# The lag between GpSimd's product and ScalarE's cast in the stick-breaking branch, from 1.5 to 3.0 units

## The chip, the cores and the metric

The kernel runs on one core of a Trainium2 chip. A core has five engines that work side by side, each through its own queue in order: TensorE (PE in the profile; its weight loads are listed as PEld), VectorE (DVE), ScalarE (ACT), GpSimd (POOL) and SyncE (SP), whose queue here issues nearly all DMAs. TensorE writes its results to PSUM, eight banks of 128 x 512 float32; the other data lie in SBUF. The metric is the time of one execution in device microseconds (us), as the median of several runs.

## The reference

One layer of a streaming encoder, for 2048 new frames of one stream (the prompt: 16 tiles of 128 rows) and 16 next frames of each of 8 running streams (the sample: one more tile of 128 rows, with 512 cached positions per stream). After an RMS norm with a conditioning vector, one wide matrix product makes queries, keys, values and gates for two attention branches. Branch A is a differential softmax attention with 4 heads; branch B is a stick-breaking attention with 8 heads of width 64. Both outputs are gated, projected and summed, and a last projection and norm follow. The lines that matter here are those of branch B:

```python
z = einsum('bqhd,bkhd->bhqk', q, k) * HEAD_DIM_B ** -0.5
mask = kpos[None, :] < qpos[:, None]
log_1m = where(mask, log_sigmoid(-z), 0.0)
log_a = log_sigmoid(z) + cumsum(log_1m, axis=3, reverse=True) - log_1m
a = where(mask, exp(log_a), 0.0)
o = einsum('bhqk,bkhd->bqhd', a, v)
```

So the weight of key k for query q is sigmoid(z) at k, times the product of sigmoid(-z) over all later keys that the query may see. The kernel computes it in that form: two sigmoids, a running product from the right, and one multiplication. Results are float32; matrix operands are split into two float16 halves, high and low, and multiplied in two or three passes.

## The kernel before

**Stages.** A first stage makes the modulated input (to about 80 us). Then come eight units: unit u has branch A for even u and branch B for odd u, and the pair u // 2 of heads (one wide head of A, two heads of B). A unit has 17 tiles: the sample's tile first (it is only projected here, and scored in the last stage), then the 16 prompt tiles in order. For each tile there is a projection (24 matmuls of 128 x 512 in 12 pieces, L467; in odd units another 24 for the gates, L543) and the scores against all keys up to the tile's own, in chunks of 512 keys (L708, L709, with the mask L712 on the last chunk). A last stage, from about 1770 us, gates, projects and stores, and scores the sample's tile beside that.

**One head of branch B in one tile.** `scores` (L694) goes through the chunks from the right. TensorE makes a chunk of z in one of three banks of PSUM that carry the tag s. ScalarE makes sigmoid(z) into the buffer sc_p and sigmoid(-z) in place in PSUM (`evacuate`, L606 and L607; by their helper, the profile has them at L134). VectorE scans sigmoid(-z) from the right into sc_n (`stick`, L682), which ends the chunk's use of the bank. A head's keys are cut into segments of up to 1024 (SEG blocks of 128): one segment in tiles 0 to 7, two in tiles 8 to 15. When the last chunk of a head has been scanned, `stick_weights` (L684) is called, first for the later segment if there are two, then for the other:

- GpSimd multiplies sc_p by the shifted sc_n into sc_p (L688, "GpSimd's product");
- `turn` (L609) follows, called some time later: ScalarE casts sc_p to float16 into sc_n's room (L616, "the cast"), VectorE subtracts that cast from sc_p to get the low half (L619, "the subtraction"), and SP issues a DMA that transposes both halves into a buffer wt (L626);
- `turn` also dates the products of these weights with the values on TensorE (`pv`, L779: L769 and L770 for branch B, L765 to L767 for branch A), 27 units (PV_LAG) after itself; the last of them for a tile ends with `natural` (L738; its last product on GpSimd is L752) and a store of the output.

There are six buffers sc_p and six sc_n (SC_BUFS), five wt (WT_BUFS), and 23 tiles of values (V_BUFS), shared by both branches. Branch A uses the same `turn` from `softmax_pair` (L632), with lags of its own (TURN_LAG, EXP_LAG, SUM_LAG).

**What sets the order.** The main loop (L1417) goes through (unit, tile) steps. For each it lists pieces of projections, about five tiles ahead (LEAD), the chunks of scores, and side work (loads and splits of the next unit's weights, sums over the caches), mixes the three lists by their costs, and hands them to `give` (L796). `give` calls one piece after another and adds its cost to a counter of the work that TensorE has been given: 0.44 (PIECE) for a projection piece of two matmuls, twice 0.22 (CHUNK) for a full chunk, 0.085 (PV_B) for a block of the weights' product in branch B. `later_on(lag, fn)` puts a function on a list that is sorted by counter + lag, and `give` calls it when the counter has got there:

```python
def later_on(lag, fn, cost=0.0):
    spent[1] += 1
    bisect.insort(due, (spent[0] + lag, spent[1], cost, fn))
...
    fn()
    spent[0] += weight * costs[i]
    while due and due[0][0] <= spent[0]:
        _, _, cost, product = due.pop(0)
        product()
        spent[0] += cost
```

So a lag counts work given to TensorE in program order, not time. The program is then handed to a scheduler that fixes each engine's queue when the program is built, by an estimate of the times; it may move an instruction ahead of others of its engine, except where the program asks for its order to be kept. The cast of the units before the last is kept in that way (L617, L618), and activations that go through the helper `act` keep their order among themselves. The subtraction and the DMA are not kept.

Unit 7 and the sample's tile call `turn` at once after the product, with no lag (L689).

Of the kernel before, what the change touches and what calls it, by code (L numbers as in the profile page):

```python
# [39 lines left out]
SEG = 8  # L40
PV_LAG = 27.0
TURN_LAG = 1.5
B_LAG = 1.5
EXP_LAG = 1.0
SUM_LAG = 2.0
PIECE, CHUNK, PV_A, PV_B = 0.44, 0.22, 0.17, 0.085
# [78 lines left out]
def layer_kernel(ctx: ExitStack, tc: tile.TileContext, a: dict):  # L125
# [483 lines left out]
    def turn(job, seg, scale=None):  # L609

        nb = seg["hi"] - seg["lo"]
        nk = nb * P
        w16 = seg["n"].bitcast(F16)
        hi, lo, src = w16[:, 0:nk], w16[:, nk : 2 * nk], seg["p"][:, 0:nk]
        if scale is None:
            x = S.copy(out=hi, in_=src)  # L616
            if job["t"] < NT and job["U"]["u"] < 7:  # L617
                kept(x)  # L618
            V.tensor_tensor(out=lo, in0=src, in1=hi, op=ALU.subtract)  # L619
        else:  # L620
            split(hi, lo, src, scale, S)
        if job["t"] == NT:
            seg["wt"] = job["pool"].tile([P, 10, P], F16, tag="dwt", name="dwt", bufs=2)
        else:
            seg["wt"] = wtp.tile([P, 2 * SEG, P], F16, tag="wt", name="wt", bufs=WT_BUFS)
        nc.sync.dma_start_transpose(out=seg["wt"][:, 0 : 2 * nb, :], in_=w16[:, 0 : 2 * nk])  # L626
        if job["t"] < NT:
            cost = (PV_A, PV_B)[job["U"]["kind"]]
            for fn in pv(job, seg):
                later_on(PV_LAG, fn, cost)  # L630
# [54 lines left out]
    def stick_weights(job, seg, later):  # L685
# [5 lines left out]
        else:  # L691
            later_on(B_LAG + m / 1024, lambda: turn(job, seg))

# [80 lines left out]
# [4 lines that stand above are left out]
# [858 lines left out]
```

## Time and profile before

| | |
|---|---|
| median of 3 runs | 2220.72 us (2216.34 to 2229.65) |
| the profiled execution, its own time | 2225.32 us |
| its span, from the first to the last instruction | 2223.5 us |
| mean granted TensorE clock | 0.980 |
| GpSimd's product L688 (units 1, 3, 5, 7) | 192 times, 313.3 us, mean 1635 ns |
| the cast L616 | 192 times, 155.0 us, mean 809 ns |
| the subtraction L619 | 192 times, 217.7 us, mean 1137 ns |
| VectorE's scan L682 | 192 times over 512 columns after another chunk (245.4 us), 128 times as a head's first (104.0 us) |

How to read the rows of the profile. A row that names one instruction in order of time has its start in us from the span's start, its duration in us, the engine, the line, the operation, what it writes <- what it reads, its shape, the count of instructions merged into the row, and in square brackets how long the engine had been idle before it and what ended that. A row of waits has the engine and line that waited, <- whom it waited for, the us in total, the times and the longest. A row that groups instructions has their count, the busy us, the mean in ns, and after the second bar the idle us before them, with what ended most of it. A row of a window has its ends, its length, the busy us of PE, PEld, DVE, ACT and POOL (each with a count), the granted TensorE clock, the share of the DMA engines and GB/s. Matmuls are pipelined and their ends are modelled, so their busy times overlap; spans on GpSimd are rough. On the page, the five busy times with their shares of the span come first.

### The profile page before, as it was taken

What the parts mean: (1) busy time and instruction counts of PE and PEld (TensorE: products, weight loads), DVE (VectorE), ACT (ScalarE), POOL (GpSimd) and SP (SyncE); (2) the same over time, 40 slices, a digit from 0 to 9 for tenths busy, and PEclk for the clock granted to TensorE, in tenths of its full rate; (3) what the DMA queues carried; (4) which work ended last, traced back from release to release, by engine and by line L of the source; (5) the groups of instructions that cost most, each with busy time, mean ns of one, the idle gap of its engine ahead of it and who ended that gap; (6) DMA issues with size and microseconds to landing.
All of it is one profiled execution on the core that took longest, in us unless ns stands there. A gap on an engine that the chain in (4) does not pass through costs nothing. (4 is left out here: it accounts for less than half of the span.)

```text
span 2223.5 us, 41495 instructions
## 1 busy us (share of the span) xinstructions
PE 2061.2 (93%) x14608; PEld 1110.4 (50%) x14608; DVE 1743.8 (78%) x3799; ACT 1606.2 (72%) x3212; POOL 699.6 (31%) x608
## 2 busy tenths in 40 slices
PE   5999999999999999999999998989998788899997
PEld 3655555555555455555554554555454444444443
DVE  4667869789887788988778888777789877787864
ACT  3978677789877677978677788876688666666531
POOL 1232014356410443742024355301334412111210
PEclk8999999999999999999999999999999899999999
DMA  9778559899796889979879999985787999999762
GB/s 323 258 241 201 120 139 217 181 227 203 200 252 158 222 201 202 207 205 221 198 195 216 191 224 207 241 181 130 159 170 155 201 280 255 230 254 224 194 166 67
DMA packets 824978, 451.05 MB, mean 203 GB/s; under 512 B 556122, under 2 KB 763274, under 8 KB 824256
## 3 DMA queue, kind: packets, MB, share of 16 engines
q1 hardware_dynamic: 823820, 448.01, 82.7%
q8 instruction: 114, 1.87, 0.3%
q14 instruction: 96, 0.79, 0.1%
q10 hardware_dynamic: 948, 0.39, 0.1%
HBM read 229.87 MB, written 86.02 MB: 142 GB/s over the span
## 5 line engine op out<-in xcount | busy, mean ns | idle before, releaser
L688 POOL TENSOR_TENSOR sc_p<-sc_p,sc_n 128x127 f32<-128x127 f32 (+7 forms) x192 | 313.3, 1635 | 663.1 <-DVE sc_n L682 510.6
L467 PEld LDWEIGHTS <-hs 128*128 128x128 f16 x3120 | 293.3, 99 | 318.5 <-issue 6.4
L467 PE MATMUL ps_mm<-wa,hs 128*128 128x512 f16 x1590 | 391.2, 382 | 5.3 <-DMA hs<-hT_d 5.0
L467 PE MATMUL ps_mm<-wb,hs 128*128 128x512 f16 x1530 | 377.4, 380 | 0.0
L682 DVE TENSOR_TENSOR_SCAN sc_n<-ps_s,sc_n,zero_t 128x512 f32<-128x512 f32 x192 | 245.4, 1278 | 33.3 <-ACT ps_s L134 28.1
L708 PE MATMUL ps_s<-k,qst 128*128 128x512 f16 (+3 forms) x640 | 223.2, 350 | 30.0 <-DVE sc_n L682 22.8
L543 PEld LDWEIGHTS <-hs 128*128 128x128 f16 x1632 | 155.0, 98 | 181.7 <-DVE qst L576 5.1
L543 PE MATMUL ps_t<-wa,hs 128*128 128x512 f16 x1020 | 242.3, 380 | 2.1 <-DVE qst L576 2.0
L619 DVE TENSOR_TENSOR sc_n<-sc_p,sc_n 128x128 f16<-128x128 f32 (+7 forms) x192 | 217.7, 1137 | 32.9 <-ACT sc_n L616 32.3
L134 ACT ACTIVATE sc_p<-ps_s,usc 128x512 f32<-128x512 f32 (+3 forms) x320 | 203.9, 637 | 34.4 <-PE ps_s L709 23.0
L709 PE MATMUL ps_s<-k,qst 128*128 128x512 f16 (+3 forms) x640 | 223.6, 350 | 0.0
L616 ACT CAST sc_n<-sc_p 128x128 f16<-128x128 f32 (+7 forms) x192 | 155.0, 809 | 57.3 <-POOL sc_p L688 55.8
L134 ACT ACTIVATE ps_s<-ps_s,usc 128x512 f32<-128x512 f32 (+3 forms) x320 | 196.3, 613 | 0.0
L543 PE MATMUL ps_t<-wb,hs 128*128 128x512 f16 x612 | 151.7, 383 | 4.8 <-DMA hs<-hT_d 2.1
L769 PE MATMUL ps_o<-v,wt 128*128 128x128 f16 x1088 | 135.2, 224 | 22.1 <-DMA wt<-sc_n 21.9
L1535 PE MATMUL ps_o<-wo,wb 128*128 128x512 f16 x624 | 141.6, 382 | 1.1 <-ACT wb L1309 1.1
L602 DVE TENSOR_SCALAR_CACHE_REDUCE sc_p<-ps_s,usc 128x512 f32<-128x512 f32 (+3 forms) x160 | 106.2, 664 | 35.7 <-PE ps_s L709 20.5
L770 PE MATMUL ps_o<-v,wt 128*128 128x64 f16 x1088 | 127.1, 196 | 0.0
L769 PEld LDWEIGHTS <-wt 128*128 128x128 f16 x1088 | 101.0, 100 | 50.1 <-DMA wt<-sc_n 25.3
L682 DVE TENSOR_TENSOR_SCAN sc_n<-ps_s,zero_t 128x128 f32<-128x128 f32 (+3 forms) x128 | 104.0, 813 | 27.7 <-ACT ps_s L134 27.7
L1501 PEld LDWEIGHTS <-wa 128*128 128x128 f16 x816 | 77.7, 98 | 94.2 <-issue 4.1
L1544 POOL TENSOR_TENSOR x<-m,x 128x512 f32<-128x512 f32 x32 | 45.6, 1427 | 247.1 <-DVE m L1539 138.7
(378 smaller groups left out, 4548.6 us busy)
## 6 DMA issues: line engine op xcount, KB each, us to landing
hs<-hT_d SPq DMA_DIRECT2D x132, 512.0 KB
g_d<-gt SPq DMA_DIRECT2D x68, 256.0 KB
out_dram<-pr SPq DMA_DIRECT2D x204, 64.0 KB
o_d<-o SPq DMA_DIRECT2D x136, 64.0 KB
wa<-g_d SPq DMA_DIRECT2D x17, 512.0 KB
wb<-g_d SPq DMA_DIRECT2D x17, 512.0 KB
hs<-o_d SPq DMA_DIRECT2D x17, 512.0 KB
wide<-in_w_ada_dram SPq DMA_DIRECT2D x8, 1024.0 KB
```

The lines of the kernel that those rows point to most:

```text
L134: i = S.activation(**kw)
L467: T.matmul(box["p"], box["h"][:, hi, k, :], U["w"][k][:, wi, :], start=(n == 0), stop=(n == 3 * KT - 1))
L543: x = T.matmul(box["g"][:, 0:gw], box["h"][:, hi, k, :], U["wg"][k // per][:, k % per, wi, :], start=(j == 0), stop=(j == 3 * KT - 1))
L616: x = S.copy(out=hi, in_=src)
L619: V.tensor_tensor(out=lo, in0=src, in1=hi, op=ALU.subtract)
L682: V.tensor_tensor_scan(out=dst[:, lo : lo + n][:, ::-1], data0=src[:, 0:n][:, ::-1], data1=zero_t[:, 0:1].to_broadcast([P, n]), initial=fi ...
L688: G.tensor_tensor(out=p[:, 0:m], in0=p[:, 0:m], in1=n[:, 1 : m + 1], op=ALU.mult)
L708: T.matmul(p[:, 0:n], qst[:, c, :], kk[:, c, 0:n], start=True, stop=False)
L709: T.matmul(p[:, 0:n], qst[:, 2 + c, :], kk[:, c, 0:n], start=False, stop=not diag)
L769: T.matmul(po[:, c * P : (c + 1) * P], wt[:, wj, :], vt[:, c, :, :], start=first, stop=False)
L770: T.matmul(po[:, c * P : c * P + 64], wt[:, nb + wj, :], vt[:, c, 0, :], start=False, stop=last)
L1535: T.matmul(po, st["y"][:, yi * 8 + k, :], wo[j * 4 + k // 2][:, wi, k % 2, :], start=(n == 0), stop=(n == 3 * KT - 1))
```

## The change

One constant, B_LAG, goes from 1.5 to 3.0:

```diff
 PV_LAG = 27.0
 TURN_LAG = 1.5
-B_LAG = 1.5
+B_LAG = 3.0
 EXP_LAG = 1.0
 SUM_LAG = 2.0
```

It is used in one place, in `stick_weights`, where m is the width of the segment (up to 1024):

```python
G.tensor_tensor(out=p[:, 0:m], in0=p[:, 0:m], in1=n[:, 1 : m + 1], op=ALU.mult)
if job["t"] == NT or job["U"]["u"] == 7:
    turn(job, seg)
else:
    later_on(B_LAG + m / 1024, lambda: turn(job, seg))
```

For a full segment `turn` is now called when TensorE has been given 4.0 units of work after the product was issued, where it was 2.5. It concerns units 1, 3 and 5. The work itself is the same.

## The prediction

> **What bounds the kernel now.** I read the busy times of the page first, then the stages by windows, then the waits of the engines inside the stages that the change touches, and last the timeline around one stall.
>
> ```profile
> PE 2061.2 (93%) x14608; PEld 1110.4 (50%) x14608; DVE 1743.8 (78%) x3799; ACT 1606.2 (72%) x3212; POOL 699.6 (31%) x608
> ```
>
> TensorE is the fullest engine. The changed constant acts only in units 1, 3 and 5 (unit 7 and the sample tiles turn their weights at once), so the three stages in which these units are scored are what matters. The next rows are those stages: length, then busy time of PE, PEld, DVE, ACT and POOL.
>
> ```profile
> 302.00:545.00 243.00, 235.06 (x1700) 128.03 (x1699) 207.16 (x350) 200.32 (x418) 115.68 (x94) 0.99 0.88 203
> 706.00:950.00 244.00, 231.49 (x1682) 126.52 (x1681) 206.68 (x345) 198.62 (x411) 117.63 (x96) 0.99 0.90 205
> 1120.00:1365.00 245.00, 230.47 (x1661) 125.37 (x1661) 206.06 (x345) 198.76 (x411) 117.37 (x96) 0.99 0.93 207
> ```
>
> TensorE stands idle for 7.94, 12.51 and 14.53 us in them, 34.98 us in all. That is the most that any change inside these stages can win by better order, whatever ScalarE's waits add up to. Who ends those idle times (total, times, longest), a fence for each of the three windows:
>
> ```profile
> PE ps_s L708 <- DVE sc_n L682: 4.8, 4, 1.7
> PE ps_s L235 <- DVE sc_n L682: 1.4, 2, 1.2
> ```
> ```profile
> PE ps_s L708 <- DVE sc_n L682: 4.4, 4, 1.7
> PE ps_s L235 <- DVE sc_n L682: 2.8, 3, 1.8
> ```
> ```profile
> PE ps_s L708 <- DVE sc_n L682: 4.4, 4, 1.7
> PE ps_s L235 <- DVE sc_n L682: 2.7, 2, 1.7
> ```
>
> So 20.5 us of the 34.98 end with VectorE's scan, which frees a bank of PSUM. And the wait that the change is aimed at, in the same windows:
>
> ```profile
> ACT sc_n L616 <- POOL sc_p L688: 15.0, 11, 2.9
> ```
> ```profile
> ACT sc_n L616 <- POOL sc_p L688: 12.1, 11, 2.5
> ```
> ```profile
> ACT sc_n L616 <- POOL sc_p L688: 12.0, 11, 2.5
> ```
>
> ScalarE stands at the cast 33 times for 39.1 us, 1.18 us each. This is no sum of time lost: ScalarE has about 43 us of slack in each stage (243.00 less 200.32), and only what reaches TensorE counts. The place where it does, in unit 3, engine by engine (PE, POOL, ACT, DVE):
>
> ```profile
> 892.53 0.38 PE L709 MATMUL ps_s<-k,qst 128*128 128x512 f16 x1
> 897.83 0.32 PE L708 MATMUL ps_s<-k,qst 128*128 128x384 f16 x1 [1.47 <-DVE sc_n L682]
> 899.41 0.38 PE L708 MATMUL ps_s<-k,qst 128*128 128x512 f16 x1 [0.95 <-DVE sc_n L682]
> ...
> 890.90 2.82 POOL L688 TENSOR_TENSOR sc_p<-sc_p,sc_n 128x1024 f32<-128x1024 f32 x1 [1.85 <-DMA g_d<-gt]
> ...
> 893.75 1.04 ACT L616 CAST sc_n<-sc_p 128x1024 f16<-128x1024 f32 x1 [1.23 <-POOL sc_p L688]
> 894.70 0.68 ACT L134 ACTIVATE sc_p<-ps_s,usc 128x512 f32<-128x512 f32 x1
> ...
> 894.83 1.75 DVE L619 TENSOR_TENSOR sc_n<-sc_p,sc_n 128x1024 f16<-128x1024 f32 x1 [1.92 <-ACT sc_n L616]
> 896.51 1.27 DVE L682 TENSOR_TENSOR_SCAN sc_n<-ps_s,sc_n,zero_t 128x512 f32<-128x512 f32 x1
> ```
>
> Read it from the bottom up. TensorE had the scores ready by 892.9. Their sigmoid stands behind the cast on ScalarE's queue and starts at 894.70; the cast waited 1.23 us for GpSimd. On VectorE the subtraction stands ahead of the scan, waits 1.92 us for the cast and takes 1.75. The scan starts at 896.51, and TensorE, out of banks, loses 1.47 and then 0.95 us: **2.42 us** from one cast placed too early. The same pair stands in units 1 and 5 (its first stall here; I take the second alike):
>
> ```profile
> 488.39 0.32 PE L708 MATMUL ps_s<-k,qst 128*128 128x384 f16 x1 [1.47 <-DVE sc_n L682]
> ```
> ```profile
> 1311.29 0.32 PE L708 MATMUL ps_s<-k,qst 128*128 128x384 f16 x1 [1.48 <-DVE sc_n L682]
> ```
>
> **The change part by part.** It removes and adds no instruction. It puts the call of turn later in the program, by 1.5 units of given-out work. What a unit is: two projection matmuls count 0.44.
>
> ```profile
> 928.10 2.97 PE L467 MATMUL ps_mm<-wb,hs 128*128 128x512 f16 x13
> 930.91 0.22 PE L769 MATMUL ps_o<-v,wt 128*128 128x128 f16 x1
> ```
>
> Thirteen take 2.81 us, 0.216 each, 0.43 for two: a unit is about 1 us of TensorE's work. A full segment's cast now follows its product by 2.5 us and would follow it by 4.0.
>
> ```profile
> L688 POOL TENSOR_TENSOR sc_p<-sc_p,sc_n 128x1024 f32<-128x1024 f32 x64 | 138.3, 2161 | 161.0 <-DVE sc_n L682 156.0 <-DVE k L323 3.1 <-DMA g_d<-gt 1.9
> ```
>
> From the last scores to the end of a product go a pair of sigmoids (0.68 each at most, by the chain above), a scan (1.27) and the product (2.16): 4.8 us, an estimate from these rows. Against 2.5 that explains why casts arrive early; against 4.0 it leaves 0.8, less ScalarE's own backlog.
>
> *What moves.* 48 casts in each of three units (16 in tiles 0 to 7, 32 in tiles 8 to 15), 144 in all; as many subtractions on VectorE; as many transposing DMAs on SP's queue; and the products of weights and values on TensorE, since turn also dates them, 27 units after itself. On GpSimd's queue turn puts nothing; only the small product of L752 that ends a tile's output moves with TensorE's. ScalarE is busy 200.32 of 243.00 us, so some 1.24 us of its work, about two sigmoids, goes ahead of a cast. The mean wait of 1.18 us is then covered; of the longest, 2.9, some 1.4 stays.
>
> *The gain.* In the quoted chain the sigmoid could start when the engine was free, at 892.5 in place of 894.70 (893.75 less the idle 1.23), and the scan 2 us earlier. That is more than the 1.47, and the 0.95 after it hangs on the same scan. Three stages at 2.42 us: **7.3 us**. The other waits at casts I value at nothing, since no idle time of TensorE follows them: its other work covers them, and if it did not, they would show among the 20.5 us. What is late next is the scan itself, on a VectorE that is the second fullest engine here.
>
> *What I leave at nothing though it ends on the scan.* The longest stall of another kind, in unit 3:
>
> ```profile
> 754.83 0.72 ACT L318 ACTIVATE wa<-wb,sw 128x512 f16<-128x512 f32 x1 [3.38 <-DMA keys_ak<-wa]
> ...
> 757.72 0.38 PE L235 MATMUL ps_s<-cacc,ones 128*128 128x1 f32 x2 [1.80 <-DVE sc_n L682]
> ```
>
> Here ScalarE waited 3.38 us for a buffer that a DMA was still reading, not for a product. The lag does not touch that, so most of the L235 rows stay.
>
> *The DMAs and SP's queue.* A transposing DMA is already held back often (first row, SP's own waits), and TensorE waits for transposes at the ends of the stages (the other rows, windows 545 to 706, 950 to 1120 and 1365 to 1542):
>
> ```profile
> SPq L626 <- PE ps_o L770: 59.2, 34, 5.4
> ```
> ```profile
> PE ps_o L769 <- DMA wt<-sc_n: 1.8, 1, 1.8
> ```
> ```profile
> PE ps_o L769 <- DMA wt<-sc_n: 4.2, 1, 4.2
> ```
> ```profile
> PE ps_o L769 <- DMA wt<-sc_n: 3.3, 1, 3.3
> ```
>
> The first row: SP waits 34 times for a product of an older segment to free one of the five wt buffers. The others: after each B stage TensorE waits once for its last transposes. Transposes and products move by the same 1.5, so the distance between them is kept, and loads for the next tile get past the transposes on SP, which is no loss to TensorE. I value this at 0. From both sides: if the last segments of a unit lose their 1.5 us against the A unit's work, +4.5 over three ends; if the loads that now pass them in time end those waits, −9.3 (the sum of the three rows).
>
> *The buffers.* sc_n is held until its transpose has read it, and there are six. The tightest reuse that I found among the scores' segments in these stages:
>
> ```profile
> 1214.97 6.71 SPq L626 DMA_TRANSPOSE wt<-sc_n  x2
> ...
> 1225.47 1.27 DVE L682 TENSOR_TENSOR_SCAN sc_n<-ps_s,sc_n,zero_t 128x512 f32<-128x512 f32 x1
> ```
>
> The two transposes are issued by 1221.68, and the next scan into the first one's buffer starts at 1225.47: at least 3.8 us of margin for a move of 1.5. Price 0; no row excludes up to +4.5 if it fails once in a stage.
>
> *The sum* against the profiled execution: 2225.32 − 7.3 = 2218.0. That execution lies 4.6 us above the median of the three runs shown, so against the median: 2220.72 − 7.3 = **2213.4 us**, 0.33% faster. A measurement of this kernel can tell about 0.5%, 11.1 us, from no change, so this would hardly be seen.
>
> **The rivals.**
>
> *All stalls that end on the scan go.* If casts at the wrong place set the whole rhythm of ScalarE and VectorE, the 20.5 us go: 2200.2 us. For it: 22 of the 33 waits fall in the two later stages, where TensorE is idle most. Against it: the L235 row above has another cause.
>
> *Nothing happens.* The order on each engine is fixed when the program is built, by a scheduler that starts from program order; it may leave the casts about where they were, or the 2.42 us may come back at another cast. For it: the waits are 39.1 us on an engine with slack, and of them only 7.3 reach TensorE. 2220.7 us.
>
> *Slower: the later subtraction lands in front of a scan that frees a bank.* The mechanism is the one quoted, in other places: VectorE takes its queue in order, and each subtraction now stands 1.5 us later, where the next tile's scans are. One such place costs 2.42 us. There are 48 heads in tiles 8 to 15 of the three units. If eight get it and the three known places stay, +19.4: 2240.1 us. It decides from five new ones on (11.1 / 2.42 = 4.6). For it: VectorE is the second fullest engine, and the subtraction is dear when it falls badly:
>
> ```profile
> L619 DVE TENSOR_TENSOR sc_n<-sc_p,sc_n x192: 258/1204/3020, 305.9 to 1756.0; 128x1024 f16<-128x1024 f32 x80, 128x128 f16<-128x128 f32 x16, 128x256 f16<-128x256 f32 x16, 128x384 f16<-128x384 f32 x16
> ```
>
> The median over all sizes is 1.20 us, the longest 3.02. [...]
>
> **How the numbers follow.** The forecast has 0.45 (own range 2207 to 2221), the large gain 0.20, no effect 0.15, the slower rival 0.20. From 2200 to 2235 the range leaves out about half of the large gain's cases and half of the slower rival's, 2 in 10 together; it holds the −9.3 and +4.5 us of the unit ends and the +4.5 of the buffers. Faster by over 0.5% (below 2209.6): most of the large gain and a little of the forecast, 0.24. Slower by over 0.5% (above 2231.8): 0.16. Within: 0.60.
>
> **What would show it.** Right: the row ACT sc_n L616 <- POOL sc_p L688 falls from 39.1 to under 15 us in the three windows; the pair of 1.47 and 0.95 us is gone in each of them; TensorE's idle time in them falls by about 7 us; the waits for wt at the ends of the stages stay within 2 us each. Wrong: the waits at the cast go and TensorE's idle time does not fall (no effect); L708 or L235 waits for L682 more often than 12 and 7 times, behind an L619 (the slower rival); or TensorE waits longer for wt, which would mean that transposes and products did not move together.

## The result, and the profile after

The changed kernel takes 2235.7 us (median of 7 runs, 2230.7 to 2242.2) against 2222.5 us (7 runs, 2216.3 to 2229.7): **slower by 0.57%**, ratio 1.0057 with a 95% interval of 1.0042 to 1.0072. The forecast was 0.33% faster. The profiled execution took 2242.2 us, 6.5 above its median; its span is 2240.4 us. First the busy times of the changed kernel:

```profile
PE 2072.4 (93%) x14608; PEld 1114.5 (50%) x14608; DVE 1728.7 (77%) x3799; ACT 1601.5 (71%) x3212; POOL 689.8 (31%) x608
```

TensorE runs the same 14,608 matmuls in both kernels, but is busy 2072.4 us in place of 2061.2. Of the 16.9 us between the two spans 11.2 are matmuls that took longer, and only 5.7 are more idle time (168.0 against 162.3). The granted clock is 0.973 against 0.980. The prediction had no term for this; it comes up again below. The tables that follow compare these two executions, one of each kernel, so differences of a few us between them are within what executions of one kernel spread over.

Next, where the time went. Each stretch below runs from the first scores of a unit to the first scores of the next (the long rows: units 1, 3 and 5), and from there to the scores of tile 4 (the short rows: the start of units 2, 4 and 6). Columns: length, busy time of PE, PEld, DVE, ACT and POOL, granted clock, DMA share, GB/s. The kernel before:

```profile
300.40:530.80 230.40, 222.46 (x1581) 120.42 (x1580) 194.72 (x311) 187.75 (x388) 107.97 (x86) 0.99 0.87 200
530.80:558.40 27.60, 25.76 (x228) 15.14 (x226) 26.57 (x68) 22.99 (x56) 17.97 (x19) 1.00 0.94 206
704.50:940.30 235.80, 223.29 (x1587) 121.07 (x1586) 198.73 (x321) 190.45 (x392) 110.09 (x88) 0.99 0.90 205
940.30:971.90 31.60, 27.42 (x228) 15.75 (x226) 28.07 (x70) 23.28 (x56) 17.91 (x19) 0.95 0.93 195
1118.30:1354.90 236.60, 223.30 (x1587) 121.00 (x1586) 198.72 (x321) 190.39 (x392) 110.29 (x88) 0.99 0.92 208
1354.90:1385.30 30.40, 25.92 (x228) 14.99 (x225) 27.58 (x72) 25.54 (x60) 18.07 (x19) 1.00 0.93 191
```

The changed kernel, the same stretches:

```profile
299.30:526.70 227.40, 222.13 (x1595) 120.07 (x1594) 194.79 (x312) 186.41 (x387) 105.21 (x87) 1.00 0.87 200
526.70:560.00 33.30, 25.47 (x202) 13.98 (x200) 26.79 (x72) 23.10 (x54) 17.92 (x19) 0.95 0.86 189
710.40:945.70 235.30, 225.65 (x1599) 123.07 (x1598) 192.98 (x322) 188.32 (x391) 106.38 (x88) 0.99 0.90 204
945.70:976.90 31.20, 26.14 (x202) 15.16 (x200) 25.69 (x66) 22.84 (x54) 18.99 (x19) 0.89 0.79 173
1128.40:1362.90 234.50, 224.67 (x1599) 121.82 (x1598) 192.38 (x322) 188.61 (x393) 105.80 (x87) 0.99 0.91 209
1362.90:1402.60 39.70, 30.78 (x224) 16.15 (x225) 28.56 (x73) 29.91 (x68) 21.83 (x23) 0.96 0.93 219
```

The three B stretches are 5.6 us shorter (697.2 against 702.8): TensorE is idle 9.0 us less in them (24.8 against 33.8) and busy 3.4 us more, with 38 more matmul records. The three starts of an A unit, which the forecast valued at nothing, are 14.6 us longer (104.2 against 89.6), although they hold 56 records fewer. The other 7.9 us of the 16.9 lie outside these stretches: the rests of units 2 and 4 are 9.4 us longer together, the time to the first scores of unit 1 is 1.1 shorter, and all behind tile 4 of unit 6 is 0.4 shorter. What TensorE waits for at the start of unit 2 in the changed kernel:

```profile
535.56 0.23 PE L769 MATMUL ps_o<-v,wt 128*128 128x128 f16 x1 [2.85 <-DMA wt<-sc_n]
538.50 0.23 PE L769 MATMUL ps_o<-v,wt 128*128 128x128 f16 x1 [1.13 <-DMA wt<-sc_n]
550.21 0.23 PE L769 MATMUL ps_o<-v,wt 128*128 128x128 f16 x1 [3.85 <-DMA wt<-sc_n]
```

Three waits for transposed weights, 7.8 us, where the kernel before had one of 1.84. The two waits at casts and at scans that the forecast was about, in the three B stages of the changed kernel (300.9 to 541, 711.9 to 955 and 1130 to 1375), ScalarE first:

```profile
ACT sc_n L616 <- POOL sc_p L688: 10.2, 6, 2.4
```
```profile
ACT sc_n L616 <- POOL sc_p L688: 7.5, 7, 1.9
```
```profile
ACT sc_n L616 <- POOL sc_p L688: 7.9, 8, 1.9
```
```profile
PE ps_s L708 <- DVE sc_n L682: 0.6, 1, 0.6
```
```profile
PE ps_s L708 <- DVE sc_n L682: 2.0, 1, 2.0
```
```profile
PE ps_s L708 <- DVE sc_n L682: 2.2, 2, 1.6
```

The casts' waits for GpSimd fell from 39.1 to 25.6 us, and TensorE's at L708 for the scan that frees a bank from 13.6 to 4.8. The stall of 1.47 and 0.95 us is gone in all three units. So the aimed-at mechanism worked, and the kernel still became slower.

### The profile page after: what moved, and what is told of

The parts are those of the page before. It is cut to its first block, busy times and chain, and to the rows that moved or that the text cites. A ratio compares the mean times of both kernels' runs of the same rounds, so it can differ in the third digit from the quotient of the medians.

```text
span 2240.4 us, 41491 instructions
## 1 busy us (share of the span) xinstructions
PE 2072.4 (93%) x14608; PEld 1114.5 (50%) x14608; DVE 1728.7 (77%) x3799; ACT 1601.5 (71%) x3212; POOL 689.8 (31%) x608
## 4 chain that ended last, share of the span: by engine, by line
PE 43%; DVE 16%; DMA 15%; ACT 12%; issue 8%; POOL 4%; SPq 2%; DVEq 0%; ACTq 0%; POOLq 0%
PE ps_mm L467 14%; PE ps_t L543 11%; DMA wt<-sc_n 4%; PE ps_o L1535 3%; PE ps_s L708 3%; PE ps_s L709 3%; DVE sc_n L682 2%; PE ps_mm L1501 2%; ACT sc_p L134 2%; ACT junk L298 2%; POOL sc_p L688 2%; DMA o_d<-o 1%; ACT ps_s L134 1%; ACT sc_n L616 1%; DMA hs<-o_d 1%
## 5 line engine op out<-in xcount | busy, mean ns | idle before, releaser
L688 POOL TENSOR_TENSOR sc_p<-sc_p,sc_n 128x127 f32<-128x127 f32 (+7 forms) x192 | 307.9, 1607 | 670.5 <-DVE sc_n L682 529.9
L467 PE MATMUL ps_mm<-wa,hs 128*128 128x512 f16 x1590 | 391.3, 381 | 11.5 <-DMA hs<-hT_d 11.0
L682 DVE TENSOR_TENSOR_SCAN sc_n<-ps_s,sc_n,zero_t 128x512 f32<-128x512 f32 x192 | 245.5, 1278 | 44.4 <-ACT ps_s L134 39.3
L708 PE MATMUL ps_s<-k,qst 128*128 128x512 f16 (+3 forms) x640 | 224.1, 351 | 22.5 <-DVE sc_n L682 14.8
L619 DVE TENSOR_TENSOR sc_n<-sc_p,sc_n 128x128 f16<-128x128 f32 (+7 forms) x192 | 215.0, 1121 | 18.3 <-ACT sc_n L616 16.8
L769 PE MATMUL ps_o<-v,wt 128*128 128x128 f16 x1088 | 131.9, 223 | 31.1 <-DMA wt<-sc_n 31.0
L508 POOL TENSOR_TENSOR rot<-pr,rope 128x256 f32<-128x256 f32 x68 | 58.7, 864 | 243.6 <-ACT pr L481 164.5
L682 DVE TENSOR_TENSOR_SCAN sc_n<-ps_s,zero_t 128x128 f32<-128x128 f32 (+3 forms) x128 | 104.3, 815 | 35.5 <-ACT ps_s L134 32.3
```

Source lines behind the costliest of these rows:

```text
L467: T.matmul(box["p"], box["h"][:, hi, k, :], U["w"][k][:, wi, :], start=(n == 0), stop=(n == 3 * KT - 1))
L682: V.tensor_tensor_scan(out=dst[:, lo : lo + n][:, ::-1], data0=src[:, 0:n][:, ::-1], data1=zero_t[:, 0:1].to_broadcast([P, n]), initial=fi ...
L688: G.tensor_tensor(out=p[:, 0:m], in0=p[:, 0:m], in1=n[:, 1 : m + 1], op=ALU.mult)
L708: T.matmul(p[:, 0:n], qst[:, c, :], kk[:, c, 0:n], start=True, stop=False)
L769: T.matmul(po[:, c * P : (c + 1) * P], wt[:, wj, :], vt[:, c, :, :], start=first, stop=False)
```

## The experiments

Eighteen kernels. The loss was first put down to SyncE's queue (theory **QUEUE**), because of this stretch of the changed kernel at the end of unit 1; VectorE's subtractions first, then SyncE's issues:

```profile
519.78 1.94 DVE L619 TENSOR_TENSOR sc_n<-sc_p,sc_n 128x1024 f16<-128x1024 f32 x1
522.94 1.23 DVE L619 TENSOR_TENSOR sc_n<-sc_p,sc_n 128x1024 f16<-128x1024 f32 x1 [0.23 <-ACT sc_n L616]
```
```profile
523.56 1.02 SPq L523 DMA_DIRECT2D out_dram<-rot  x2
...
525.57 1.71 SPq L462 DMA_DIRECT2D rope<-in_shapes_dram  x1
...
528.85 4.62 SPq L626 DMA_TRANSPOSE wt<-sc_n  x1
...
534.19 1.67 SPq L626 DMA_TRANSPOSE wt<-sc_n  x1
```

The subtractions end at 521.72 and 524.17, and their transposes are issued 7.1 and 10.0 us later, behind stores and loads. QUEUE says that this makes the last weights of a unit late. Its rivals: **HELD**, products dated later that hold buffers of the next unit; and **REDRAWN**, that a moved date makes the scheduler write a new order on every engine, whose time has little to do with the move.

The results in one table. TensorE has 28,319 matmuls and weight loads in the built program, the same ones in every kernel here. "Lines" is how many of them have to be taken out of the order of the kernel before and put in elsewhere to get the order of the other kernel (line of the kernel, tiles without their running numbers, shapes and offsets compared); the last column is the ratio to runs of the kernel before on the same chip (medians 2217.2 to 2218.8 us, 11 to 23 runs; 2222.5 for the changed kernel).

| kernel | lag of the casts in units 1, 3, 5 | lines | us | ratio (95%) |
|---|---|---|---|---|
| one_cast | 3.0 for one cast a unit | 723 | 2220.7 | 1.0017 (1.0006 to 1.0028) |
| u5_only | 3.0 in unit 5 | 1,401 | 2220.4 | 1.0010 (0.9993 to 1.0027) |
| pv_268 | 1.5; products 26.8 | 2,788 | 2230.8 | 1.0055 (1.0033 to 1.0077) |
| one_and_last | one cast 3.0, tile 15 1.0 | 2,862 | 2239.5 | 1.0095 (1.0082 to 1.0109) |
| pv_272 | 1.5; products 27.2 | 2,903 | 2227.5 | 1.0039 (1.0023 to 1.0055) |
| pv_kept | 3.0; products as before | 3,414 | 2230.8 | 1.0057 (1.0036 to 1.0078) |
| lag_225 | 2.25 | 4,014 | 2243.0 | 1.0107 (1.0086 to 1.0127) |
| one_cast_25 | 2.5 for one cast a unit | 4,143 | 2240.6 | 1.0096 (1.0078 to 1.0114) |
| the change | 3.0 | 4,271 | 2235.7 | 1.0057 (1.0042 to 1.0072) |
| t13_only | 3.0 in tile 13 | 4,421 | 2248.3 | 1.0135 (1.0116 to 1.0155) |
| lag_16 | 1.6 | 4,481 | 2247.9 | 1.0130 (1.0108 to 1.0152) |
| less_15 | 1.5; less work on ScalarE | 4,848 | 2229.0 | 1.0055 (1.0039 to 1.0071) |
| st_pool_15 | 1.5; stores on GpSimd | 4,893 | 2272.4 | 1.0241 (1.0224 to 1.0259) |
| st_pool_30 | 3.0; stores on GpSimd | 5,126 | 2245.1 | 1.0120 (1.0104 to 1.0137) |
| l3_pv268 | 3.0; products 26.8 | 5,227 | 2235.7 | 1.0093 (1.0073 to 1.0113) |
| not_last | 3.0, tiles 14 and 15 1.5 | 5,412 | 2240.7 | 1.0109 (1.0089 to 1.0128) |
| lag_45 | 4.5 | 5,489 | 2236.1 | 1.0077 (1.0056 to 1.0098) |
| l3_pv272 | 3.0; products 27.2 | 5,656 | 2239.0 | 1.0105 (1.0085 to 1.0125) |
| less_30 | 3.0; less work on ScalarE | 6,304 | 2228.7 | 1.0048 (1.0030 to 1.0067) |

### Other sizes of the same move

```diff
-B_LAG = 1.5
+B_LAG = 1.6      # lag_16;  2.25: lag_225;  4.5: lag_45
```

lag_16: 

> The lag is 1.6 in place of 1.5, a tenth of a unit (0.1 us of TensorE's work). Three theories of why lag 3.0 came out 13 us slower. QUEUE: the later transposes stand behind loads and stores on SyncE's queue, so wt is late at the ends of the B units; a shift of 0.1 us cannot do that, so the time stays within 2 us of the kernel before (2220 to 2225 us). HELD: the products of weights and values, dated from the turn, come later and hold buffers that the next unit needs; the same 2220 to 2225 us. REDRAWN: any moved date makes the scheduler write another order on every engine, and the time of that order has little to do with the size of the move; then it may differ by as much as lag 3.0 did, 5 to 15 us either way.

lag_225: 

> Lag 2.25, half of the move. QUEUE and HELD: between the two kernels, about half of the loss, and the stalls of tile 13 gone or halved: 2222 to 2232 us. REDRAWN: no relation to the size, 2212 to 2240 us.

lag_45: 

> Lag 4.5, the move doubled. QUEUE: the loss doubles, 2240 to 2260 us, with more than 31 us of waits for wt. REDRAWN: no relation to the size, 2225 to 2250 us. If the later cast is worth something of itself, which the row of 2247.9, 2243.0 and 2235.7 us at 1.6, 2.25 and 3.0 hints at, it comes out at or below 2236 us.

Measured 2247.9, 2243.0 and 2236.1 us. Moves of 0.1, 0.75, 1.5 and 3.0 units cost 30.7, 25.8, 13.2 and 17.3 us. QUEUE and HELD need a price that grows with the move; the smallest move is the dearest. In lag_45 the last six transposes of unit 1 follow their subtractions by 0.0 to 2.4 us, where in the changed kernel it was 5.4 to 10.0 and in the kernel before 0.2 to 4.7: the very stretch that QUEUE pointed at is better than in the kernel before, and the kernel is slower all the same. REDRAWN says nothing of how the sizes rank, and its figure for lag_16, 5 to 15 us, was too small.

### Parts of the change

```diff
-            later_on(B_LAG + m / 1024, lambda: turn(job, seg))
+            later_on((3.0 if job["t"] == 13 else B_LAG) + m / 1024, lambda: turn(job, seg))            # t13_only
+            later_on((3.0 if job["U"]["u"] == 5 else B_LAG) + m / 1024, lambda: turn(job, seg))        # u5_only
+            later_on((3.0 if job["t"] < 14 else 1.5) + m / 1024, lambda: turn(job, seg))               # not_last
```

pv_kept has B_LAG 3.0 and this:

```diff
-                later_on(PV_LAG, fn, cost)
+                later_on(PV_LAG - (1.5 if job["U"]["kind"] == 1 and job["U"]["u"] < 7 else 0.0), fn, cost)
```

t13_only: 

> Lag 3.0 in tile 13 of units 1, 3 and 5 alone, where the three stalls of 1.47 and 0.95 us stood; 1.5 elsewhere. The stalls with the half-clock stretch behind each were worth 8.0 us in the profiles (2.6, 2.6 and 2.8 us in the stretches that hold them). QUEUE and HELD: the gain is kept and nearly all of the loss goes, since the last two tiles of each unit keep their dates: 2213 to 2217 us. REDRAWN: the pairs may go, but the total is as much up to chance as before, 2212 to 2235 us, and losses show in places that tile 13 does not touch.

pv_kept: 

> Lag 3.0 for the turns of units 1, 3 and 5, but their products of weights and values are dated 25.5 units after the turn in place of 27, so that they keep the dates of the kernel before. HELD: the loss goes and the gain stays, 2212 to 2218 us. QUEUE: the transposes are as late as in the changed kernel and the products wait for them sooner, so it is as slow or slower, 2234 to 2245 us, with more than the 18.8 us of waits for wt in the three B stages. REDRAWN: neither, anywhere from 2212 to 2240 us.

u5_only: 

> Lag 3.0 in unit 5 alone. The stretch from tile 12 of unit 5 to the first scores of unit 6 was 2.8 us shorter in the changed kernel. Until unit 5 the order is that of the kernel before. REDRAWN: units 1 to 4 as before, 2 to 5 us won at tile 13 of unit 5, then a new order in units 6 and 7 that gives back 0 to 15 us: 2215 to 2235 us in all. QUEUE: one third of the gain and one third of the loss: 2223 to 2226 us, with the loss at the waits for wt as unit 6 begins (4.5 us before, 5.6 and 3.2 for a load of h after).

not_last: 

> Lag 3.0 in tiles 0 to 13 of units 1, 3 and 5, lag 1.5 in tiles 14 and 15. QUEUE: the last transposes go ahead of the next unit's loads again, the waits for wt in the three B stages fall from 18.8 to about 10 us, the gain at tile 13 stays, and the time is 2212 to 2220 us. REDRAWN: the waits may fall, but the total stays at 2222 to 2240 us.

Measured 2248.3, 2230.8, 2220.4 and 2240.7 us. HELD falls: with the products at their old dates the loss is still 13.6 us. QUEUE falls a second time: in not_last the waits for wt at the starts of units 2, 4 and 6 are 3.9, 3.3 and 1.1 us, 8.3 together against 10.5 in the kernel before (1.84, 4.18, 1.22 and 3.26), and the kernel is 22.4 us slower. t13_only moves 12 of the 144 casts and loses 31.1 us, more than the whole change; u5_only moves 48, its order is that of before until unit 5, and it loses nothing that can be measured. Yet in the stretches of units 5 and 6 as many lines are redrawn as by the change (569 and 715 in both). So a new order need not cost anything, and the loss of the change is not shown to lie there.

### The date of something else

```diff
-PV_LAG = 27.0
+PV_LAG = 27.2    # pv_272, l3_pv272;  26.8: pv_268, l3_pv268 (the l3 kernels with B_LAG 3.0)
```

pv_272: 

> The lag of the casts stays 1.5; the products of weights and values are dated 27.2 units after the turn in place of 27.0, in all units. Nothing of the change is in it. After the first four runs (lag 1.6 was 30.7 us slower, lag 2.25 25.8 us, lag 3.0 in tile 13 alone 31.1 us, products kept 13.6 us) the theory REDRAWN says: the kernel before is a lucky order, and any other order costs 10 to 30 us, this one too: 2227 to 2250 us. LAG, the rival: what costs is something that every larger lag of the cast does at once, above 1.5; then this kernel stays within 5 us of 2220.

pv_268: 

> The same step the other way: products dated 26.8 units after the turn, casts at lag 1.5. REDRAWN: 2227 to 2250 us, again slower although the step goes the other way. LAG: within 5 us of 2220; if the date of the products were what matters, one of the two would be faster and the other slower by about the same.

l3_pv272: 

> Lag 3.0 with the products dated 27.2 units after the turn; to be set against the same step at lag 1.5 (2227.5 us). REDRAWN: the lag has no price of its own and the four orders at lag 3.0 lie where the two at lag 1.5 lie, 2222 to 2236 us. If lag 3.0 costs 13 us of itself: 2241 us (2227.5 + 13).

l3_pv268: 

> Lag 3.0 with the products dated 26.8 units after the turn; to be set against the same step at lag 1.5 (2230.8 us). REDRAWN: 2222 to 2238 us. If lag 3.0 costs 13 us of itself: 2244 us (2230.8 + 13).

Measured 2227.5 and 2230.8 us at lag 1.5: 8.7 and 12.0 us slower, for a fifth of a unit in either direction, with no cast moved. That is nearly the price of the change (13.2). At lag 3.0 they took 2239.0 and 2235.7 us; the first is above the 2236 that REDRAWN allowed and near the 2241 of a lag that costs 13 us of itself. So beside equal dates of the products lag 3.0 was dearer by 13.2, 11.5 and 4.9 us; three draws, which left open whether a price of the lag stands on top of the price of the new order.

### Work taken off a queue or an engine

st_pool_15 and st_pool_30 issue the stores of keys, values and z from GpSimd:

```diff
-            load(out=out_rows(nk, t, h * P, P), in_=rot[:, 128:256])
+            nc.gpsimd.dma_start(out=out_rows(nk, t, h * P, P), in_=rot[:, 128:256])
...
```

less_15 and less_30 let ScalarE square 128 of 1024 columns in the sums beside the stages, so most of those sums are left out. They try a fourth theory, **FULL SCALARE**: ScalarE's work at the end of a unit sets when the last casts, and with them the last weights, are ready.

```diff
-            sum_squares(st, 1024, dst, scale=scale, keep=True)
+            sum_squares(st, 128, dst, scale=scale, keep=True)
...
```

st_pool_15: 

> Lag 1.5, with the stores of keys, values and z (three of a tile's loads and stores) issued by GpSimd in place of SyncE; nothing is left out. For the pair with the next kernel. QUEUE: SyncE has some 350 issues fewer, the waits for wt fall in both kernels, and lag 3.0 no longer costs: the two within 5 us of one another. If SyncE's queue is not what makes lag 3.0 dear, the two stay 5 to 13 us apart. The level of both is open: GpSimd's products wait behind its issues, 2210 to 2260 us.

st_pool_30: 

> The same stores on GpSimd's queue at lag 3.0. QUEUE: within 5 us of the kernel at lag 1.5, with waits for wt in the three B stages near 10 us in place of 18.8. Not QUEUE: 5 to 13 us slower than it.

less_15: 

> Lag 1.5; the sums of squares of weights and caches that ScalarE takes beside the stages read 128 of 1024 columns, so seven eighths of those sums are left out and the output is not the reference's. In the last 45 us of unit 1 that frees about 4.5 us of ScalarE (six such instructions of 1.07 us). FULL SCALARE: the last cast of each B unit comes 3 to 5 us sooner after the scores of tile 12 than the 87.8, 87.8 and 89.0 us of before, and the kernel is 8 to 20 us faster, 2198 to 2210 us, although TensorE's work is the same. If TensorE or the DMAs set the ends of the units, the time stays at 2218 to 2232 us.

less_30: 

> Lag 3.0 with the same work left out. FULL SCALARE: with slack on ScalarE the won stalls count, and lag 3.0 is 3 to 9 us faster than lag 1.5 with the same work left out. QUEUE: it stays 5 to 13 us slower than that kernel, with transposes 5 us and more behind their subtraction at the ends of the units. REDRAWN: within 10 us either way.

Measured 2272.4 (above the 2210 to 2260 that were thought possible) and 2245.1 us, 2229.0 and 2228.7 us. With the stores off SyncE, lag 3.0 is 27.3 us faster than lag 1.5; with less work on ScalarE the two are 0.3 us apart. Over the five pairs that differ in the lag alone it costs +13.2, +11.5, +4.9, −27.3 and −0.3 us: no price that stays from one order to the next. Five pairs that scatter so widely can't exclude one of a few us. QUEUE, which wanted the first pair within 5 us, falls a third time: in st_pool_30 five of unit 1's last six transposes follow their subtraction at once (0.0 us) and one by 0.5, and the kernel takes 2245.1 us. FULL SCALARE fails as a forecast of the time: in less_15 the last cast came 2.1, 2.2 and 1.5 us sooner after the scores of tile 12 (85.7, 85.6 and 87.5 us), and the kernel was 10.3 us slower, not 8 to 20 faster. That does not clear ScalarE, since the orders of less_15 and less_30 differ from the start on. Less work in a new order was slower than more work in the old one.

### One cast

one_cast moves one cast in each of units 1, 3 and 5, the one behind which the 2.42 us stood; one_cast_25 moves the same cast by less, to lag 2.5; one_and_last adds lag 1.0 in tile 15.

```diff
-            later_on(B_LAG + m / 1024, lambda: turn(job, seg))
+            later_on(B_LAG + (1.5 if job["U"]["u"] < 7 and (job["t"], job["c"]) == (13, 0) and later is not None else 0.0) + m / 1024, lambda: turn(job, seg))
```

one_cast: 

> Lag 3.0 for one cast in each of units 1, 3 and 5: that of tile 13, first head, blocks 0 to 7, behind which the 1.47 and 0.95 us stood. On ScalarE it moves past one pair of sigmoids; most of the order of the kernel before stays on all engines. If the mechanism of the forecast is right and the loss comes from the order elsewhere, the three pairs go and with them the half-clock stretch that followed each: 3 x (2.42 + up to 1.7), 7.3 to 12.4 us faster, 2206 to 2212 us. If the pair only moves to another cast, the time stays at 2219 within 4 us. If any new order costs 10 us or more, it is 2222 to 2240 us.

one_cast_25: 

> Lag 2.5 in place of 3.0 for the one cast per unit of one_cast (tile 13, first head, blocks 0 to 7); lag 1.5 elsewhere. By the lag alone it lies between before and one_cast, 2218 to 2221 us. REDRAWN: the stalls of 1.47 and 0.95 us go here as well, and still the time is that of another order, 5 to 30 us above before: 2224 to 2249 us, with the loss in places that the cast does not touch.

one_and_last: 

> The moved cast of one_cast, and lag 1.0 for all turns of tile 15 in units 1, 3 and 5. If the last transposes set the start of the next unit: the last waits for wt (2.33, 3.61 and 3.07 us in one_cast) shrink by up to 0.5 us each and most of the 9.3 us counts, 2210 to 2215 us. REDRAWN: its order differs by some 14,000 lines on TensorE, so 2220 to 2245 us.

Measured 2220.7, 2240.6 and 2239.5 us. one_cast was to take 2206 to 2212 us if the forecast's mechanism was right and the loss lay elsewhere, and it did not get there.

At lag 3.0 the order of ScalarE's instructions changes at that place by this alone ("-" before, "+" one_cast):

```
-L616 CAST sc_n<-sc_p 128x1024
-L134 ACTIVATE sc_p<-ps_s,usc_2861 128x512
-L134 ACTIVATE ps_s<-ps_s,usc_2861 128x512
+L134 ACTIVATE sc_p<-ps_s,usc_2861 128x512
+L134 ACTIVATE ps_s<-ps_s,usc_2861 128x512
+L616 CAST sc_n<-sc_p 128x1024
```

The timeline of one_cast there, in unit 1:

```profile
479.88 2.82 POOL L688 TENSOR_TENSOR sc_p<-sc_p,sc_n 128x1024 f32<-128x1024 f32 x1 [1.85 <-DVE sc_n L682]
...
482.73 1.04 ACT L616 CAST sc_n<-sc_p 128x1024 f16<-128x1024 f32 x1
...
486.81 0.38 PE L708 MATMUL ps_s<-k,qst 128*128 128x512 f16 x1 [0.87 <-DVE sc_n L682]
```

The product ends at 482.70, the cast starts at 482.73 and waits for nothing, and of 2.42 us of TensorE's stall 0.87 is left (0.86 in units 3 and 5). Now the same six stretches for one_cast:

```profile
299.60:526.10 226.50, 220.69 (x1583) 119.45 (x1582) 194.31 (x309) 185.50 (x383) 105.14 (x86) 1.00 0.86 202
526.10:558.40 32.30, 27.73 (x228) 16.15 (x225) 29.63 (x72) 25.20 (x60) 19.00 (x20) 0.95 0.94 205
703.70:936.10 232.40, 221.35 (x1587) 119.89 (x1586) 198.81 (x319) 188.39 (x389) 107.57 (x88) 1.00 0.89 207
936.10:970.40 34.30, 28.78 (x228) 16.37 (x226) 30.33 (x75) 25.01 (x58) 18.66 (x20) 0.90 0.95 197
1117.20:1350.10 232.90, 221.81 (x1587) 119.96 (x1586) 198.26 (x319) 188.06 (x387) 108.29 (x88) 1.00 0.92 209
1350.10:1384.20 34.10, 28.16 (x229) 16.08 (x226) 28.91 (x75) 27.59 (x64) 19.36 (x20) 0.95 0.96 194
```

The B stretches add up to 691.8 us, 11.0 less than before (5.8 of it idle time of TensorE, 5.2 its busy time), and the starts of the A units to 100.7, 11.1 more. **The gain is there, and as much is given back within the next four tiles.** These are again one execution of each kernel, and the two spans, 2218.6 and 2223.5 us, differ the other way from the medians on one chip, 2220.7 and 2218.3; the medians decide that nothing was won. TensorE comes to the first scores of unit 2 at 526.1 in place of 530.8, and then waits for the last transposes of unit 1:

```profile
547.60 0.29 PE L769 MATMUL ps_o<-v,wt 128*128 128x128 f16 x1 [2.33 <-DMA wt<-sc_n]
...
958.56 0.29 PE L769 MATMUL ps_o<-v,wt 128*128 128x128 f16 x1 [3.61 <-DMA wt<-sc_n]
...
1373.15 0.23 PE L769 MATMUL ps_o<-v,wt 128*128 128x128 f16 x1 [3.07 <-DMA wt<-sc_n]
```

In the kernel before the same products ran at 549.11, 960.91 and 1375.97:

```profile
549.11 0.23 PE L769 MATMUL ps_o<-v,wt 128*128 128x128 f16 x1 [1.84 <-DMA wt<-sc_n]
...
960.91 0.23 PE L769 MATMUL ps_o<-v,wt 128*128 128x128 f16 x1 [4.18 <-DMA wt<-sc_n]
...
1375.97 0.23 PE L769 MATMUL ps_o<-v,wt 128*128 128x128 f16 x1 [3.26 <-DMA wt<-sc_n]
```

TensorE was 4.7, 4.2 and 4.8 us earlier (0.8, 0.8 and 1.1 of it already at the start of the stage), the products, and so the transposes that they waited for, only 1.5, 2.4 and 2.8. What paces those last transposes is not settled: ScalarE, SyncE's queue and the dates of tile 15 were each tried, and each trial came with a new order that cost more than it could show.

one_cast_25 is the sharpest pair of the study. The same cast, moved by 1.0 in place of 1.5: 4,143 lines in place of 723, and 2240.6 us in place of 2220.7. The two run the same instructions. By their profiles TensorE is busy 8.4 us longer (2072.5 against 2064.1) and idle 12.8 us longer (167.3 against 154.5). Where this is lost can't be read from one stretch, as tiles 0 to 7 of unit 3 show, the kernel before first and then one_cast_25:

```profile
704.50:791.20 86.70, 79.38 (x571) 44.24 (x570) 67.93 (x149) 64.41 (x145) 32.67 (x31) 1.00 0.81 202
```
```profile
701.00:799.70 98.70, 91.29 (x618) 49.66 (x617) 73.33 (x159) 73.54 (x159) 34.73 (x32) 0.97 0.77 192
```

The stretch is 12.0 us longer, but 47 more matmul records stand in it and TensorE is idle as long as before (7.4 and 7.3 us): it is work that the old order had done elsewhere, and no loss. one_and_last took 2239.5 us where its theory asked for 2210 to 2215. REDRAWN is left, but it gave no sizes: lag_16, lag_225, t13_only, not_last and l3_pv272 came out above the ranges that it had named.

## Why the prediction was wrong, point by point

- **The step that failed** is the list of what moves. It said of the change that it removes and adds no instruction and puts the call of turn later in the program, and it priced 144 casts, their subtractions, transposes and products, with everything else left standing. What the runs show in its place: no instruction came or went, but from the first moved date on the scheduler put the work of all engines in another order, 4,271 of 28,319 lines on TensorE, 2,563 of them in the stretches of units 2, 4, 6 and 7, whose own casts the constant does not reach. The rival "nothing happens" had the scheduler in it, but only as something that might leave the casts where they were.
- **The size of the new order's price**: the 16 other kernels with 2,788 lines and more, a tenth of all, are all slower than before, by 8.7 to 53.8 us (the 53.8 with its stores moved as well); the two with 723 and 1,401 lines are within 2.4 us. The two kernels that only shift the products' date by 0.2 cost 8.7 and 12.0. The change's ratio, 1.0057 (1.0042 to 1.0072), is that of pv_268, 1.0055 (1.0033 to 1.0077), in which nothing of the change stands. Beyond that the number of lines does not tell the price: less_30 has the most and costs 10.0 us. That the order sets the time is shown by one_cast against one_cast_25; which property makes the order of before better than the 17 that differ widely from it stays open, and so does which part of the new order costs the change its 13.2 us.
- **The stall of 2.42 us a unit** was read rightly: it is gone in the changed kernel and cut to 0.87 us in one_cast, and moving that one cast past one pair of sigmoids is enough. In the changed kernel TensorE's idle time in the B stretches fell by 9.0 us, where about 7 was the mark. Seen by length the term was too small: the three B stretches of one_cast are 11.0 us shorter, not 7.3: in the kernel before 3.4 us at half clock followed each of the three (from 490.3, 899.9 and 1312.9, below), and the granted clock of these stretches is 1.00 in one_cast in place of 0.99; only 5.8 of the 11.0 are idle time. A stall of 1.69 or 1.70 us behind the scan in the last tile of each B unit, too, stood in no term, and the changed kernel has lost it.
- **The unit ends at nothing** (bounds −9.3 and +4.5) was the term with the wrong size: the starts of the A units are 14.6 us longer in the changed kernel and 11.1 in one_cast, and the waits for wt there came to 7.8, 5.1 and 5.6 us, where 2 each was the mark. Transposes and products were dated together, as the step said, but on the chip they did not stay together: TensorE waits longer for wt, the sign that the prediction itself named, and the last six transposes of unit 1 follow their subtractions by 5.4 to 10.0 us in place of 0.2 to 4.7. In one_cast, with most of the order kept, TensorE is earlier by what it won and reaches products whose weights are less early than it is. A stall was taken out of an engine that had to wait later in any case.
- **The waits at the casts** fell to 25.6 us, not below 15. The prediction valued them at nothing, and no run shows that they cost anything. The matmuls of L235, whose waits were mostly to stay, wait for the scan no more at all (6.9 us in the whole kernel before). The moved casts were not expected to touch them; that the new order did it is likely, but no run isolates it.
- **The slower rival** gave the right sign, but not by its mechanism: it needed more waits for the scan, and TensorE waits 14 times for L682 at L708 in the whole changed kernel (14.8 us), 25 times before (22.8). The subtractions did not get dearer either (215.0 us in all, 217.7 before). That the sign came right is luck.
- **The clock** was missing. Of the 16.9 us between the two profiles 11.2 are the same matmuls taking longer, at a granted clock of 0.973 in place of 0.980.

What decided the sign, how good the order of before is among those that the same scheduler would write, stands in no row of its trace.

## What to carry to other kernels

Where a scheduler fixes the order at build time, a changed date is not a local edit: first compare the two built orders, and if they differ far beyond the place of the edit, price the new order by a control that shifts something unrelated as little, before crediting the edit with anything. A stall taken from the fullest engine counts only as far as the next wait behind it moves too (in one_cast 11.0 us were won in the B stretches and 11.1 lost in the four tiles behind them); follow the chain to where the next unit begins. To test a mechanism, look for the smallest edit that leaves the rest of the order as it was (here one cast of 144 moved past two instructions).

## What the runs showed of the hardware that was not expected

**Two stalls of 1.47 and 0.95 us cost their length and then 3.4 us at half clock.** Windows of 3.4 us of the kernel before; the columns are as above, and the granted clock is the third number from the end:

```profile
486.90:490.30 3.40, 0.99 (x8) 0.59 (x7) 3.26 (x6) 3.29 (x8) 2.36 (x2) 1.00 0.98 182
490.30:493.70 3.40, 3.40 (x26) 2.35 (x24) 3.40 (x6) 3.40 (x9) 2.74 (x3) 0.50 0.64 143
...
640.50:643.90 3.40, 1.82 (x10) 0.82 (x8) 0.62 (x4) 3.40 (x12) 0.00 (x0) 1.00 1.11 193
643.90:647.30 3.40, 3.02 (x38) 2.34 (x39) 3.40 (x8) 2.76 (x6) 0.00 (x0) 1.00 0.91 223
```

And of the changed kernel:

```profile
547.70:551.10 3.40, 0.89 (x20) 0.90 (x21) 3.37 (x6) 2.00 (x4) 3.40 (x4) 1.00 0.82 180
551.10:554.50 3.40, 3.40 (x14) 1.40 (x12) 3.40 (x6) 2.42 (x6) 0.57 (x1) 0.51 0.38 83
...
643.30:646.70 3.40, 1.47 (x9) 0.62 (x6) 0.81 (x4) 3.40 (x11) 0.00 (x0) 1.00 1.10 103
646.70:650.10 3.40, 2.36 (x17) 1.80 (x18) 3.36 (x9) 2.30 (x4) 0.00 (x0) 0.50 1.02 263
650.10:653.50 3.40, 3.40 (x25) 2.56 (x24) 1.59 (x4) 0.88 (x1) 0.00 (x0) 0.50 1.02 336
```

The pair of 1.47 and 0.95 us fell into the window from 486.9, TensorE was busy 0.99 us in it, and the next 3.4 us ran at half clock: up to 1.7 us more. In these two traces the half-clock stretches begin on a fixed grid: 490.3, 899.9 and 1312.9 lie 120 and 121 times 3.413 us apart, which is also the length of the shortest of them. After the first 60 us the two traces have 29 such onsets, all on the grid of their trace to within 0.02 us; every window at full clock with more than 1.96 us of idle time was followed by one, none with less than 1.74 (1.58 idle at 640.5: nothing; 1.93 at 643.3: two windows at half clock). Over the traces of all twenty kernels the least idle time before an onset was 1.38 us (t13_only) and the most without one 1.99 (less_30). So what idle time cost in these traces went by where it fell on the grid: the pair of 2.42 us lay in one window, and half clock followed; the stall of 3.26 us before 1375.97 in the kernel before was split, 1.59 us of idle time in the window from 1370.9 and 1.67 in the one from 1374.3, and the clock stayed at 1.00 there and in the two windows behind. Over the span the clock withheld (1 − 0.980) × 2223.5 = 44.5 us before and (1 − 0.973) × 2240.4 = 60.5 after; by the trace's clock intervals 31.6 and 42.3 of them while TensorE was busy, 10.7 more, which is nearly the 11.2 by which the same matmuls took longer.

**A store issued by GpSimd took 0.56 us of that engine.** st_pool_15 has 344 instructions more on GpSimd, the stores, and the profile gives them 192.3 us of its time; GpSimd is busy 882.6 us in place of 699.6. It is the engine that the casts wait for, though these waits hardly grew: 56.1 us in the whole of st_pool_15, 55.8 before.
